# Attention on one core: the last-but-one head's normalisation is split over two engines, and the last full pair is stored in one piece

## The chip, the cores and the metric

The kernel runs on one core of a Trainium2 chip. The metric is the device time of one execution in microseconds (us), lower is better. The engines of a core that matter here are TensorE (PE, matrix products into PSUM), VectorE (DVE), ScalarE (ACT, here the exponentials), GpSimd (POOL, casts) and SyncE (SP), from whose queue most transfers are issued. ScalarE has such a queue too (ACTq). Each engine works through its own instructions in order and waits on semaphores for the others.

## The reference

Plain softmax attention, 8 batches of 8 heads, 512 queries and 512 keys of 64 numbers each, in float32:

```python
scale = 1.0 / np.sqrt(q.shape[-1])
scores = np.einsum('bhqd,bhkd->bhqk', q, k) * scale
scores = scores - scores.max(axis=-1, keepdims=True)
attn = np.exp(scores)
attn = attn / attn.sum(axis=-1, keepdims=True)
return np.einsum('bhqk,bhkd->bhqd', attn, v)
```

The output is 8 x 8 x 512 x 64 float32, 128 KB a head.

## The kernel before

**Tiling.** The 64 heads are handled as 32 pairs g = 0 to 31 of two heads h = 0, 1. For each pair q, k and v are loaded by one transfer of 256 KB each, cast to fp16 by GpSimd, and q and k are transposed by TensorE. The scores are made transposed, keys on the partitions, in blocks of 128 keys x 512 queries; two blocks go through one exponential on ScalarE (line 579). For 16 of the 128 groups VectorE works out the exponential instead (lines 596 to 640).

**Units.** The product with v (`values`, line 680) is made in units of 128 queries: four units a head, each 128 x 65 in PSUM, where the 65th column is the sum of the exponentials, since v has a column of ones. Units are counted from 4 in the order in which the heads are multiplied. Seven units share one PSUM tile, `os[u // 7]`, which fills one bank; I call it bank 0, 1, ... 36 by that number, although two places in PSUM take turns. When a bank is complete, `reciprocal` (line 645) takes 1 / sum for its units, and `normalise` (line 650) multiplies all its units by these in one VectorE instruction into `ring`, an SBUF buffer of 112 units. `store` (line 658) sends a head of four units from the ring to memory, as soon as it is whole. The pairs in `Plan.PAIRED` go out in one 256 KB transfer when their second head is there; the others as two of 128 KB.

**The end.** The order of the heads is such that pair 30 has units 244 to 251 and the first head of pair 31 has units 252 to 255; these four are alone in bank 36 and so are a normalisation of their own. The last head, (31, 1), does not use these banks: `last_values` (line 696) makes its four units in a tile of the scores' pool, `o_last`, and `finish` (line 705) takes their reciprocals (line 709), multiplies them into `obl` (line 710) and stores that from SP's queue (line 716). `store` sends the last two heads before it, (30, 1) and (31, 0), from ScalarE's queue (`left < 2`), all others from SP's.

**What sets the order.** `Plan` simulates the engines with costs given by hand and writes a list of steps (scores, values, rec, mul, store, finish and others), sorted by time; the kernel emits its instructions in the order of this list. The layer under it adds the semaphore waits between engines, from what each instruction reads and writes. `Plan.PAIRED` is read only by `store`, not by the planner, so that the list of steps is the same before and after the change.

Of the kernel before, what the change touches and what calls it, by code (L numbers as in the profile page):

```python
# [14 lines left out]
AluOp = mybir.AluOpType  # L15


class Plan:
# [25 lines left out]
    SCALE_PORT, PRODUCT_PORT, GAP, REACH = 271, 537, 20, 5  # L44
    FIRST_LAND, LOAD, STORE, LATENCY, ISSUE = 5200, 740, 370, 2300, 470
    QUEUED, URGENT = 3500, 16
    PAIRED = (3, 13)
    RAW, QK16, NV, NU = 7, 5, 12, 112
    PAIR, DUEK, DUEV, DUEL, PRE = 3300, 2800, 4000, 7000, 0

# [357 lines left out]
def kernel(  # L408
# [7 lines left out]
    nc = tc.nc  # L416
    B, H, S, D = q.shape
    P = 128
    NI = S // P
    assert NI == 4 and D == 64 and S == 512  # L420
    scale = float(D) ** -0.5
    NP = (B * H) // 2
    ppb = H // 2
    LAST = NP - 1
# [25 lines left out]
    NU = Plan.NU  # L450
    ring = cpool.tile([P, NU, D], FP32, name="ring")
# [9 lines left out]
    os, rcs = {}, {}  # L461
# [3 lines left out]
    last = {}  # L465

    def source(src, g):
        b, h = g // ppb, 2 * (g % ppb)
        return src[b, h : h + 2].rearrange("h (p i) d -> p h i d", i=NI)
# [12 lines left out]
    def load(g, names):  # L482
        if g >= NP:
            return
        for name in names:
            src = {"q": q, "k": k, "v": v}[name]
            t = load_tile(g, name)
            nc.sync.dma_start(out=t[:, :, :, :], in_=source(src, g))
# [24 lines left out]
    def dve(ins):  # L513
        latest[:] = [ins] + latest[: Plan.REACH]
        return ins
# [23 lines left out]
    def copy(g, n=0):  # L539
        if g == 1:  # L540
            dve(
                nc.vector.tensor_copy(
                    out=tqk[g][:, n], in_=tps[g][:, n].rearrange("p i c -> p (i c)")
                )
            )
            return
        dve(
            nc.vector.tensor_copy(  # L548
                out=tqk[g][:, :, :], in_=tps.pop(g).rearrange("p n i c -> p n (i c)")
            )  # L550
        )
# [90 lines left out]
    def reciprocal(u, n):  # L642
        rcs[u] = opool.tile([P, 7, 1], FP32, tag="rc", name=f"rc_{u}")
        o, x = os[u // 7], u % 7
        dve(nc.vector.reciprocal(out=rcs[u][:, 0:n], in_=o[:, x : x + n, D : D + 1]))  # L645

    def normalise(u, n):
        o, x = os[u // 7], u % 7
        dve(
            nc.vector.tensor_tensor(  # L650
                out=ring[:, u % NU : u % NU + n, :],
                in0=o[:, x : x + n, 0:D],
                in1=rcs.pop(u)[:, 0:n].broadcast_to([P, n, D]),
                op=AluOp.mult,
            )
        )

    def store():

        g, h, u0 = heads.pop(0)  # L660
        left = 2 * NP - 1 - (u0 + NI - Plan.FIRST_UNIT) // NI
        queue = nc.scalar if left < 2 else nc.sync
        u = u0 % NU
        if g in Plan.PAIRED and h == 0:
            return
        if g in Plan.PAIRED:
            both = ring[:, u - NI : u + NI, :].rearrange("p (h i) d -> p h i d", h=2)
            queue.dma_start(out=source(out, g), in_=both)
        else:
            queue.dma_start(out=source(out, g)[:, h], in_=ring[:, u : u + NI, :])  # L670
# [34 lines left out]
    def finish():  # L705
        o = last["o"]
        ob = opool.tile([P, NI, D], FP32, tag="obl", name="obl", bufs=1)
        rc = opool.tile([P, 7, 1], FP32, tag="rc", name="rc_last")
        nc.vector.reciprocal(out=rc[:, 0:NI], in_=o[:, :, D : D + 1])
        nc.vector.tensor_tensor(  # L710
            out=ob[:, :, :],
            in0=o[:, :, 0:D],
            in1=rc[:, 0:NI].broadcast_to([P, NI, D]),
            op=AluOp.mult,
        )
        nc.sync.dma_start(out=source(out, LAST)[:, 1], in_=ob[:, :, :])

    def first_loads():
        tk = load_tile(0, "k")
        tq = load_tile(0, "q")  # L720
        for h in range(2):
            nc.scalar.dma_start(out=tk[:, h], in_=source(k, 0)[:, h])
            nc.sync.dma_start(out=tq[:, h], in_=source(q, 0)[:, h])
# [95 lines left out]
    with tc.manual_schedule():  # L819
        plan = Plan(groups, NP, 3)  # L820
        steps = plan.run()
        first_loads()
        for g, name in plan.first_loads:
            load(g, name)
        make_identity(nc, ident)
        for n in range(NV):
            nc.vector.memset(vps[n][:, :, :, D : D + 1], 1.0)
        first_pair()
        do = {
            "transposes": transposes,  # L830
            "scores": scores,
            "values": values,
            "load": load,
            "store": store,
            "cast": cast_behind,
            "raise": raise_,
            "copy": lambda g, b: copy(g),
            "pass": pass_,
            "last": last_values,
            "finish": finish,  # L840
            "rec": lambda u, n, b: reciprocal(u, n),
            "mul": lambda u, n, b: normalise(u, n),
        }
        for what, *args in steps:
            do[what](*args)


# [28 lines left out]
```

## Time and profile before

| what | us |
|---|---|
| median of 3 runs (114.2 to 114.3) | 114.28 |
| the profiled execution | 114.39 |
| its span, first to last instruction | 112.5 |
| TensorE busy | 104.1 |
| ScalarE busy | 105.6 |
| VectorE busy | 101.2 |
| GpSimd busy | 65.2 |

The span is what the trace shows; the profiled execution is 1.9 us longer than it. Times in the rows of the trace are microseconds from the start of the span: a row of the timeline has the start, the length, the engine, the line, the operation, and what it writes and reads, with a count of instructions that were merged. A length after several merged instructions runs from the first one's start to the last one's end. A row of grouped instructions (with a vertical bar) gives the group's busy time and the mean length of one in ns, then the idle time ahead of them. The engines' names with q (ACTq, SPq) are the transfers issued there: the length is that of issuing, not of the transfer. Rows of transfers end with the size and the median us from issue to landing. A row of windows has the stretch, its length, the busy time of PE, PEld (weight loads), DVE, ACT and POOL with the count of instructions, TensorE's granted clock, the share of time in which the 16 DMA engines were busy, and GB/s.

### The profile page before, as it was taken

What the parts mean: (1) busy time and instruction counts of PE and PEld (TensorE: products, weight loads), DVE (VectorE), ACT (ScalarE), POOL (GpSimd) and SP (SyncE); (2) the same over time, 40 slices, a digit from 0 to 9 for tenths busy, and PEclk for the clock granted to TensorE, in tenths of its full rate; (3) what the DMA queues carried; (4) which work ended last, traced back from release to release, by engine and by line L of the source; (5) the groups of instructions that cost most, each with busy time, mean ns of one, the idle gap of its engine ahead of it and who ended that gap; (6) DMA issues with size and microseconds to landing.
All of it is one profiled execution on the core that took longest, in us unless ns stands there. A gap on an engine that the chain in (4) does not pass through costs nothing.

```text
span 112.5 us, 4339 instructions
## 1 busy us (share of the span) xinstructions
PE 104.1 (93%) x1687; PEld 69.4 (62%) x1687; DVE 101.2 (90%) x226; ACT 105.6 (94%) x118; POOL 65.2 (58%) x127
## 2 busy tenths in 40 slices
PE   7988889899999998999999999999999999999970
PEld 2554546576775565657677557678567765776560
DVE  1547999999989999999999999999999999999760
ACT  4689999999999999999999999999999999999960
POOL 2165798265478866686847888755868796000000
PEclk9999999999999999999999999999999999999999
DMA  3999999999999999999999999999999886848435
GB/s 99 301 304 359 349 349 345 351 340 346 348 342 335 313 326 355 349 353 365 324 359 348 319 300 328 340 339 312 337 338 283 277 267 207 269 145 273 154 100 182
DMA packets 35349, 33.84 MB, mean 301 GB/s; under 512 B 2560, under 2 KB 35328, under 8 KB 35328
## 3 DMA queue, kind: packets, MB, share of 16 engines
q1 hardware_dynamic: 34752, 33.04, 91.4%
q10 hardware_dynamic: 576, 0.52, 1.4%
q8 instruction: 13, 0.21, 0.9%
q14 instruction: 8, 0.07, 0.2%
HBM read 25.17 MB, written 8.39 MB: 298 GB/s over the span
## 4 chain that ended last, share of the span: by engine, by line
DVE 45%; PE 42%; ACT 7%; issue 2%; DMA 1%
PE o L680 18%; PE st L575 14%; DVE pd L599 10%; DVE tqk L548 8%; DVE ring L650 8%; ACT pt L579 7%; PE tp L535 6%; DVE m L633 4%; DVE pd L639 3%; PE st_0a L727 3%; DVE pe L625 3%; DVE m L616 2%; DVE m L635 2%; DVE rc L645 2%; DMA out_dram<-ring 1%
## 5 line engine op out<-in xcount | busy, mean ns | idle before, releaser
L579 ACT ACTIVATE pt<-st 128x1024 f16<-128x1024 f32 (+1 forms) x110 | 100.3, 1111 | 0.0
L680 PE MATMUL o<-vp,pt 128*128 128x65 f16 x880 | 46.3, 194 | 0.1
L680 PEld LDWEIGHTS <-pt 128*128 128x128 f16 x880 | 38.9, 98 | 12.2 <-issue 10.6
L575 PE MATMUL st<-tqk 64*128 64x512 f16 (+1 forms) x250 | 42.4, 381 | 2.9 <-ACT pt L579 1.7
L504 POOL CAST qkp<-k 128x512 f16<-128x512 f32 x31 | 21.7, 701 | 12.1 <-DMA k<-in_k_dram 5.2
L494 POOL CAST vp<-v 128x512 f16<-128x512 f32 x32 | 21.9, 700 | 7.9 <-DVE rc L645 2.9
L504 POOL CAST qkp<-q 128x512 f16<-128x512 f32 x30 | 21.4, 712 | 6.6 <-DVE rc L645 3.1
L650 DVE TENSOR_TENSOR ring<-o,rc 128x448 f32<-128x448 f32 (+2 forms) x37 | 22.3, 606 | 0.6
L680 PE MATMUL o<-vp,pe 128*128 128x65 f16 x128 | 22.1, 195 | 0.0
L680 PE MATMUL o<-vp,pd 128*128 128x65 f16 x128 | 21.9, 193 | 0.0
L548 DVE COPY tqk<-tp 128x1024 f16<-128x1024 f16 x30 | 20.3, 677 | 0.2 <-PE tp L535 0.2
L535 PE MATMUL tp<-ident,qkp 128*128 128x128 f16 x248 | 19.5, 219 | 0.9 <-DVE ring L650 0.7
L599 DVE TENSOR_SCALAR pd<-st 128x1024 uint16<-128x1024 f32 x16 | 19.5, 1217 | 0.7 <-PE st L575 0.7
L575 PEld LDWEIGHTS <-tqk 64*128 64x128 f16 x250 | 11.8, 93 | 12.3 <-issue 4.8
L535 PEld LDWEIGHTS <-qkp 128*128 128x128 f16 x248 | 14.3, 97 | 7.3 <-issue 4.1
L680 PEld LDWEIGHTS <-pe 128*128 128x128 f16 x128 | 12.5, 97 | 3.8 <-issue 2.9
L680 PEld LDWEIGHTS <-pd 128*128 128x128 f16 x128 | 12.6, 98 | 0.0
L639 DVE TENSOR_TENSOR pd<-pd,m 128x1024 f16<-128x1024 f16 x16 | 10.9, 682 | 0.0
L633 DVE TENSOR_TENSOR m<-m 128x1024 f16<-128x1024 f16 x16 | 10.9, 681 | 0.0
L645 DVE RECIPROCAL rc<-o 128x7 f32<-128x7 f32 (+2 forms) x37 | 7.2, 196 | 1.9 <-PE o L680 1.9
L625 DVE TENSOR_SCALAR pe<-pd 128x1024 uint16<-128x1024 uint16 x16 | 6.8, 422 | 0.0
L616 DVE TENSOR_SCALAR m<-pd 128x1024 uint16<-128x1024 uint16 x16 | 6.6, 412 | 0.0
(50 smaller groups left out, 34.5 us busy)
## 6 DMA issues: line engine op xcount, KB each, us to landing
v<-in_v_dram SPq DMA_DIRECT2D x32, 256.0 KB, 5.7
k<-in_k_dram SPq DMA_DIRECT2D x31, 256.0 KB, 5.8
q<-in_q_dram SPq DMA_DIRECT2D x31, 256.0 KB, 5.8
out_dram<-ring SPq DMA_DIRECT2D x57, 128.0 KB, 3.4
out_dram<-ring SPq DMA_DIRECT2D x2, 256.0 KB, 3.5
k<-in_k_dram ACTq DMA_DIRECT2D x2, 128.0 KB, 2.9
q<-in_q_dram SPq DMA_DIRECT2D x2, 128.0 KB, 2.7
out_dram<-ring ACTq DMA_DIRECT2D x2, 128.0 KB, 2.0
```

The costliest lines, as they stand in the source:

```text
L494: return nc.gpsimd.tensor_copy(out=vps[g % NV][:, :, :, 0:D], in_=raw[g]["v"][:, :, :, :])
L504: return nc.gpsimd.tensor_copy(out=dst, in_=src[:, :, :, :])
L535: reads[g] = nc.tensor.transpose(tps[g][:, n, i, :], qkp[g][:, n, i, :], ident)
L548: nc.vector.tensor_copy(out=tqk[g][:, :, :], in_=tps.pop(g).rearrange("p n i c -> p n (i c)"))
L575: nc.tensor.matmul(st[:, x, cols], kc, qc[:, cols], start=True, stop=True)
L579: nc.scalar.activation(out=pt[:, :, cols], in_=st[:, :, cols], func=EXP, scale=scale, bias=SHIFT)
L599: nc.vector.tensor_scalar(out=r["pd"][:, :, :], in0=r["st"][:, :, :], scalar1=BITS, scalar2=BIAS, op0=AluOp.mult, op1=AluOp.add,)
L625: ins = nc.vector.tensor_scalar(out=r["pe"][:, :, :], in0=u[:, :, :], scalar1=0x7C00, scalar2=None, op0=AluOp.bitwise_and,)
L633: ins = nc.vector.tensor_tensor(out=m16, in0=m16, in1=m16, op=AluOp.mult)
L639: ins = nc.vector.tensor_tensor(out=u16, in0=u16, in1=m16, op=AluOp.mult)
L650: nc.vector.tensor_tensor(out=ring[:, u % NU : u % NU + n, :], in0=o[:, x : x + n, 0:D], in1=rcs.pop(u)[:, 0:n].broadcast_to([P, n, D]), o ...
L680: nc.tensor.matmul(os[u // 7][:, u % 7, :], part[:, y * P : (y + 1) * P], vps[g % NV][:, h, c, :], start=(n == 0), stop=(n == len(parts) - 1),
```

## The change

In `normalise` the last bank's four units, 252 to 255, are no longer one instruction. ScalarE multiplies the first two, each by its own reciprocal, one instruction each. VectorE multiplies the third at once. The fourth is kept back and emitted in `finish`, between the last head's reciprocal and its multiply. Pair 30 takes the place of pair 13 in `PAIRED`: it goes out in one transfer of 256 KB, from SP's queue, since `left < 1` leaves only head (31, 0) on ScalarE's; pair 13 goes out in two transfers. The store of the last head is emitted behind all steps of the list instead of in `finish`. Lines of the changed file: 665 the ScalarE multiplies, 650 the single VectorE multiplies, 670 the multiply of a whole bank, 688 and 690 the stores, 729 and 732 `finish`, 868 the last store.

```diff
-    PAIRED = (3, 13)
+    PAIRED = (3, 30)
...
+    def one_unit(u, i):
+        def do_it():
+            dve(
+                nc.vector.tensor_tensor(
+                    out=ring[:, (u + i) % NU, :],
+                    in0=os[u // 7][:, u % 7 + i, 0:D],
+                    in1=rcs[u][:, i, :].broadcast_to([P, D]),
+                    op=AluOp.mult,
+                )
+            )
+
+        return do_it
+
     def normalise(u, n):
         o, x = os[u // 7], u % 7
+        if u + n == Plan.FIRST_UNIT + 8 * NP - NI:
+
+            for i in range(n // 2):
+                nc.scalar.mul(ring[:, (u + i) % NU, :], o[:, x + i, 0:D], rcs[u][:, i, :])
+            last["units"] = [one_unit(u, i) for i in range(n // 2, n)]
+            last["units"].pop(0)()
+            return
...
-        queue = nc.scalar if left < 2 else nc.sync
+        queue = nc.scalar if left < 1 else nc.sync
...
         nc.vector.reciprocal(out=rc[:, 0:NI], in_=o[:, :, D : D + 1])
+        for unit in last["units"]:
+            unit()
         nc.vector.tensor_tensor(
             out=ob[:, :, :],
             in0=o[:, :, 0:D],
             in1=rc[:, 0:NI].broadcast_to([P, NI, D]),
             op=AluOp.mult,
         )
-        nc.sync.dma_start(out=source(out, LAST)[:, 1], in_=ob[:, :, :])
+        last["ob"] = ob
...
         for what, *args in steps:
             do[what](*args)
+        nc.sync.dma_start(out=source(out, LAST)[:, 1], in_=last["ob"][:, :, :])
```

## The prediction

> **What bounds the kernel now.** I read the core's clock first, then the page's totals, then the timeline of each engine from 105 us on, because the change lies almost wholly behind the last exponentials.
>
> ```profile
> core 0: 112.5 us, clock 1.000
> PE 104.1 (93%) x1687; PEld 69.4 (62%) x1687; DVE 101.2 (90%) x226; ACT 105.6 (94%) x118; POOL 65.2 (58%) x127
> 106.18 0.20 DVE L645 RECIPROCAL rc<-o 128x7 f32<-128x7 f32 x1 [0.59 <-PE o L680]
> 107.94 0.20 DVE L645 RECIPROCAL rc<-o 128x7 f32<-128x7 f32 x1 [0.89 <-PE o L680]
> 108.18 0.62 DVE L650 TENSOR_TENSOR ring<-o,rc 128x448 f32<-128x448 f32 x1
> 108.72 0.17 DVE L645 RECIPROCAL rc<-o 128x4 f32<-128x4 f32 x1
> 108.92 0.42 DVE L650 TENSOR_TENSOR ring<-o,rc 128x256 f32<-128x256 f32 x1
> 109.27 0.17 DVE L709 RECIPROCAL rc_last<-o_last 128x4 f32<-128x4 f32 x1
> 109.47 0.42 DVE L710 TENSOR_TENSOR obl<-o_last,rc_last 128x256 f32<-128x256 f32 x1
> 106.51 2.11 ACT L579 ACTIVATE pt<-st 128x1024 f16<-128x1024 f32 x3
> 108.83 0.90 ACTq L670 DMA_DIRECT2D out_dram<-ring  x2
> 107.07 2.09 SPq L670 DMA_DIRECT2D out_dram<-ring  x3
> 109.92 0.33 SPq L716 DMA_DIRECT2D out_dram<-obl  x1
> 108.25 0.73 PE L696 MATMUL o_last<-vp,pt 128*128 128x65 f16 x16
> ```
>
> For 105 us TensorE, ScalarE and VectorE are all above 90% busy and the change adds nothing there but one DMA. The end is a chain on VectorE. ScalarE's last exponential ends at 106.51 + 2.11 = 108.62; TensorE's last product for the last head ends at 108.25 + 0.73 = 108.98. From 107.94 VectorE does six instructions without a hole: reciprocal and multiply of bank 35 (units 245 to 251), reciprocal and multiply of bank 36 (units 252 to 255, the last-but-one head), reciprocal and multiply of the last head. The last-head reciprocal starts at 109.27, 0.08 before the multiply ahead of it ends (108.92 + 0.42 = 109.34), and 0.29 after its own input was done. So it stands in VectorE's queue, not behind TensorE. The last multiply ends at 109.89, its store is issued at 109.92.
>
> ```profile
> 107.07 1.66 DMA out_dram<-ring
> 108.73 0.17 DVE rc L645
> ```
>
> These two rows of the chain of waits put the bank-36 reciprocal down to a store. I do not follow them: it starts 0.08 before the multiply ahead of it ends, as the last-head one does, so it stood in the same queue.
>
> ```profile
> out_dram<-ring SPq DMA_DIRECT2D x3, 128.0 KB, 2.0
> out_dram<-ring ACTq DMA_DIRECT2D x2, 128.0 KB, 2.0
> out_dram<-obl SPq DMA_DIRECT2D x1, 128.0 KB, 1.8
> 109.00:110.00 1.00, 0.00 (x0) 0.00 (x0) 0.86 (x3) 0.00 (x0) 0.00 (x0) 1.00 0.49 165
> 110.00:111.00 1.00, 0.00 (x0) 0.00 (x0) 0.00 (x0) 0.00 (x0) 0.00 (x0) 1.00 1.04 340
> 111.00:112.50 1.50, 0.00 (x0) 0.00 (x0) 0.00 (x0) 0.00 (x0) 0.00 (x0) 0.99 0.15 50
> ```
>
> The last store lands 1.8 after its issue, at 111.7, and 0.8 of barrier follows. In the windows (last two numbers: DMA share, GB/s) the transfers are full from 110 to 111 and nearly empty after: the last store runs close behind the ones before it, but is not far from free.
>
> The profiled execution took 114.39 us, 1.9 more than its span; the median of the three runs, 114.28, is 0.1 below it. I work out a shift of the span and add it to the median.
>
> **The change, part by part.**
>
> *Two units on ScalarE, one on VectorE, then the last head.* The 0.42 multiply of bank 36 goes. ScalarE gets two multiplies of 64 elements, reading bank 36 of PSUM and its reciprocals; VectorE gets one of 64 ahead of the last-head reciprocal, and one between that and the last multiply. The point on which all turns is a wait. In the changed program as built, the first single multiply on VectorE waits for ScalarE's counter at the value that the second of the two ScalarE multiplies sets; the first of the two sets nothing. So ScalarE's pair and VectorE's unit do not run side by side but one after the other, and the last-head reciprocal, in the same queue behind the waiting unit, is late with it, and so are the second unit, the last multiply and its store.
>
> [...]
>
> The price needs ScalarE and VectorE instructions of a size that the trace before lacks, so I go by its nearest rows:
>
> ```profile
> 4.02 0.41 ACT L745 CAST q<-q 128x256 f16<-128x256 f32 x1 [0.32 <-DMA q<-in_q_dram]
> 4.33 0.40 ACT L746 CAST k<-k 128x256 f16<-128x256 f32 x1
> 5.16 0.60 ACT L777 ACTIVATE pt<-st_0a 128x512 f16<-128x512 f32 x1 [0.43 <-PE st_0a L770]
> 5.66 0.59 ACT L777 ACTIVATE pt<-st_0b 128x512 f16<-128x512 f32 x1
> 107.41 1.21 ACT L579 ACTIVATE pt<-st 128x512 f16<-128x512 f32 x2
> L579 ACT ACTIVATE pt<-st 128x512 f16<-128x512 f32 x2 | 1.2, 726 | 0.0
> L579 ACT ACTIVATE pt<-st 128x1024 f16<-128x1024 f32 x108 | 99.3, 1118 | 0.0
> L743 ACT ACT_TABLE_LOAD x1 | 1.3, 1283 | 1.7 <-PEq L860 1.7
> L650 DVE TENSOR_TENSOR ring<-o,rc 128x448 f32<-128x448 f32 x35 | 21.6, 618 | 0.5
> L650 DVE TENSOR_TENSOR ring<-o,rc 128x256 f32<-128x256 f32 x1 | 0.4, 424 | 0.0
> L650 DVE TENSOR_TENSOR ring<-o,rc 128x192 f32<-128x192 f32 x1 | 0.4, 351 | 0.0
> ```
>
> VectorE: 448, 256 and 192 elements cost 618, 424 and 351 ns, about 1.03 ns an element; 64 elements come to 0.22 us. ScalarE: 512 elements take 0.60 and start 0.50 apart (5.16, 5.66), 256 take 0.40 and start 0.31 apart (4.02, 4.33). In line with these, 64 elements take 0.25 and start 0.17 apart: 0.42 for the pair. Lower end: the two late exponentials start 1.21 - 0.73 = 0.48 apart, and from 512 to 1024 elements one grows by 392 ns, 0.77 an element, so 64 would start 0.14 apart and the pair could be done in 0.14 + 0.22, say 0.33. Upper end: no overlap and the 0.40 of the cast each, 0.80. All these rows take their scale as a constant, where the multiply reads one per partition, so I take 0.46, a little above the nearest pair.
>
> [...]
>
> Now the sum. The bank-36 reciprocal ends at 108.72 + 0.17 = 108.89 as before. ScalarE has been free since 108.62 and starts 0.05 later, 108.94 (hand-overs in the first rows: multiply end 108.80 to ScalarE's DMA issue 108.83; multiply end 109.89 to SP's issue 109.92). The pair ends at 109.40. VectorE's unit starts at 109.44. Its end, 109.66, less the 0.08 by which VectorE instructions without a wait overlap, puts the last-head reciprocal at 109.58 (before: 109.27). It ends at 109.75; the second unit starts at 109.67 and ends at 109.89; the last multiply needs the reciprocal (109.75 + 0.03) and the queue (109.89 - 0.08) and starts at 109.81, where it was 109.47. **Shift: +0.34 us.** With the pair at 0.33 or 0.80 it is +0.21 or +0.68.
>
> Had the wait not been there, VectorE's first unit would start at 108.92, the reciprocal at 109.06 (its input is done at 108.98), the last multiply at 109.29: -0.18.
>
> *The stores at the end.* Before, (30,0) left on SP and (30,1) on ScalarE's queue, both when bank 35 was done (108.80), and (31,0) on ScalarE's queue behind. Now pair 30 is one 256 KB store on SP, issued at 108.83, and only (31,0) is left on ScalarE. It waits for VectorE's second unit, 109.89, is issued at 109.92 and lands 2.0 later, 111.9. The last store is issued at 109.81 + 0.42 + 0.03 = 110.26 and lands 1.8 later, 112.06: still last. The pair store lands by 111.2, if it takes 0.4 longer than the 2.0 of a single one; I cost it at nothing, covered by 0.8. That the last store is now emitted behind all steps costs nothing either: SP's queue holds only the pair store ahead of it, issued a microsecond before. Whether the last store lands in 1.8 is open: the one before it is now 0.34 ahead instead of half a microsecond, but pair 30 has drained by then. I take no change, with 0.1 either way.
>
> *Pair 13 leaves in two stores.* One more issue on SP at about 87 us:
>
> ```profile
> 87.04 0.41 SPq L668 DMA_DIRECT2D out_dram<-ring  x1
> 87.55 0.45 SPq L488 DMA_DIRECT2D v<-in_v_dram  x1
> ...
> L494 POOL CAST vp<-v x32: 607/626/1017, 9.0 to 93.8; 128x512 f16<-128x512 f32 x32
> ```
>
> Behind it in SP's queue stands the last load, v of pair 30, about 0.4 later than at 87.55. Its cast, among the last of those up to 93.8, has until the first unit of pair 30, the last unit of bank 34, whose reciprocal waits for TensorE at 106.18. Over 10 us of cover; cost nothing, and +0.4 if the cover were gone.
>
> **The rivals.** (About 0.2%, 0.23 us, is what a measurement of this kernel can tell from no change: 114.05 to 114.51 is the same.)
>
> 1. *The wait costs nothing.* ScalarE's pair would have to be done when VectorE comes to its unit, by 108.9; then the chain is 0.18 shorter: 114.10, and 114.0 if the last store also finds the transfers free. Against it: the pair cannot start before 108.89, where the reciprocals end. Only a ScalarE pair of less than about 0.12 (0.34 less of it than taken) breaks even, and the shortest pair I could draw from the rows is 0.33.
> 2. *A short pair.* At 0.33 the shift is 0.21: 114.49, told by the measurement from nothing at best barely. For it: the lower line above. Against: the scale that is read.
> 3. *The store of (31,0) becomes the late one.* It and the last store, 0.34 apart, carry 128 KB each; at the 340 GB/s of the windows that is 0.39 a store, so the second may wait 0.05 to 0.1 on the first: 114.72. For it: ScalarE's stores took 2.0, the last one 1.8.
> 4. *A table load before the first multiply*, 1283 ns as in the row: 115.9. Against: the program as built has one load, at the start.
> 5. *The stores of pair 13 delay something*: up to 114.7. Against: the cover above.
>
> **How the numbers follow.** Forecast, the serial chain: 0.66, 114.62, its own range 114.50 to 114.80. Rival 1: 0.06 (most of it faster, the rest the same); rival 2: 0.15; rival 3: 0.09; rivals 4 and 5: 0.02 each. Slower: 0.66 + 0.09 + 0.04 = 0.79; same: 0.15 and the rest of rival 1, 0.17; faster: 0.04. The range runs from 114.40 (the short pair with the last store 0.1 quicker) to 114.95 (the upper pair, 0.68); outside it are rival 1, rival 4 and the tails.
>
> **What would show it.** In the changed kernel's timeline: two ScalarE instructions of 128x64 from about 108.94, end near 109.40; VectorE's first 128x64 multiply starting only behind them, with idle time put down to ScalarE before it, where VectorE had none; the last-head reciprocal near 109.58 and the last multiply near 109.81; the last store issued near 110.26, landing after 1.8. If VectorE's first single multiply starts near 108.92, the forecast is wrong at its root. If the order holds and the time is off, it is the pair's length or the landing of the last store. Any difference before 105 us would speak for rival 5.

## The result and the profile after

| | before | after |
|---|---|---|
| median, us (22 runs each) | 114.29 | 114.71 |
| lowest to highest, us | 113.68 to 115.43 | 114.07 to 115.70 |
| ratio, 95% interval | | 1.0042, 1.0023 to 1.0062 |
| the profiled execution, us | 114.39 | 115.06 |
| its span, us | 112.5 | 113.2 |

The change costs 0.48 us by the ratio (0.26 to 0.71 by its interval). The forecast was 114.62, slower. Medians and ratios here and below leave out the executions that ran slow, two of `e5_vector_alone` (116.41 and 132.25, at a lower clock) and three of the kernel before.

The two profiled executions differ by 0.66 in span, more than the change can be charged with. The exponentials of the execution after are 0.24 later than before by 26 us and 0.26 at the last; nothing of the change has happened by 26 us, and in the executions of the other kernels this offset lies anywhere from -0.27 to +0.65 by then. So the tail is read from a mark that both kernels reach in the same way: the start of the reciprocal of bank 36, called R below (108.72 before, 108.98 after). R stands at the same distance behind the start of the last exponential, to within 0.01, in all executions profiled here but two; those two are of one kernel (`e7_early_store`, run again as `e11_early_again`), whose edit puts it 0.065 later. Where an experiment takes two reciprocals for bank 36, R is the start of the first.

First the cores view and the page's totals of the kernel after, then its timeline of VectorE, ScalarE and SyncE.

```profile
core 0: 113.2 us, clock 0.999
PE 103.4 (91%) x1687; PEld 68.5 (61%) x1687; DVE 101.1 (89%) x227; ACT 106.2 (94%) x120; POOL 65.5 (58%) x127
108.44 0.62 DVE L670 TENSOR_TENSOR ring<-o,rc 128x448 f32<-128x448 f32 x1
108.98 0.17 DVE L645 RECIPROCAL rc<-o 128x4 f32<-128x4 f32 x1
109.74 0.23 DVE L650 TENSOR_TENSOR ring<-o,rc 128x64 f32<-128x64 f32 x1 [0.59 <-ACT ring L665]
109.88 0.17 DVE L729 RECIPROCAL rc_last<-o_last 128x4 f32<-128x4 f32 x1
109.97 0.19 DVE L650 TENSOR_TENSOR ring<-o,rc 128x64 f32<-128x64 f32 x1
110.08 0.42 DVE L732 TENSOR_TENSOR obl<-o_last,rc_last 128x256 f32<-128x256 f32 x1
106.77 2.12 ACT L579 ACTIVATE pt<-st 128x1024 f16<-128x1024 f32 x3
109.19 0.52 ACT L665 ACTIVATE ring<-o,rc 128x64 f32<-128x64 f32 x2 [0.29 <-DVE rc L645]
110.24 0.34 ACTq L690 DMA_DIRECT2D out_dram<-ring  x1
109.09 0.38 SPq L688 DMA_DIRECT2D out_dram<-ring  x1
110.54 0.33 SPq L868 DMA_DIRECT2D out_dram<-obl  x1
```

The row to look at is the third of VectorE: 0.59 of idle time, ended by ScalarE. VectorE's reciprocal ends at 109.15, ScalarE's two multiplies run from 109.19 to 109.71 beside an idle VectorE, and only then the single multiply starts, at 109.74. The last head's reciprocal, in the same queue, is late with it (0.90 behind R; before 0.55), then the last multiply (1.11 behind R; before 0.75), then its store. The chain of waits now begins inside this stretch:

```profile
109.71 0.02 issue
109.74 0.23 DVE ring L650
109.96 0.09 DVE rc_last L729
110.05 0.11 DVE ring L650
110.16 0.35 DVE obl L732
```

All it has is VectorE and 0.02 of issue ahead of it; the chain stops at 109.71, the end of ScalarE's second multiply.

The last three transfers of the kernel after (operation, count, size, us from issue to landing), and then by windows of half a microsecond, the last two numbers being the DMA engines' busy share and GB/s:

```profile
out_dram<-ring SPq DMA_DIRECT2D x1, 256.0 KB, 2.1
out_dram<-ring ACTq DMA_DIRECT2D x1, 128.0 KB, 1.7
out_dram<-obl SPq DMA_DIRECT2D x1, 128.0 KB, 1.8
110.25:110.75 0.50, 0.00 (x0) 0.00 (x0) 0.26 (x1) 0.00 (x0) 0.00 (x0) 1.00 1.01 342
110.75:111.25 0.50, 0.00 (x0) 0.00 (x0) 0.00 (x0) 0.00 (x0) 0.00 (x0) 1.00 0.33 109
111.25:111.75 0.50, 0.00 (x0) 0.00 (x0) 0.00 (x0) 0.00 (x0) 0.00 (x0) 1.00 1.01 344
111.75:112.25 0.50, 0.00 (x0) 0.00 (x0) 0.00 (x0) 0.00 (x0) 0.00 (x0) 1.00 0.28 92
```

Windows of the kernel before:

```profile
109.50:110.00 0.50, 0.00 (x0) 0.00 (x0) 0.40 (x1) 0.00 (x0) 0.00 (x0) 1.00 0.65 219
110.00:110.50 0.50, 0.00 (x0) 0.00 (x0) 0.00 (x0) 0.00 (x0) 0.00 (x0) 1.00 1.03 336
110.50:111.00 0.50, 0.00 (x0) 0.00 (x0) 0.00 (x0) 0.00 (x0) 0.00 (x0) 1.00 1.05 344
111.00:111.50 0.50, 0.00 (x0) 0.00 (x0) 0.00 (x0) 0.00 (x0) 0.00 (x0) 1.00 0.45 150
```

Before, the transfers run without a hole from 110.00 until the last one is through. After, there is a hole at 110.75 to 111.25: pair 30 has gone and head (31, 0) is not there yet. Both readings come back below, with the experiments' numbers in one table (us behind R, one profiled execution each; a kernel's last landing is that of the transfer that ends last):

| kernel | last multiply starts | its store issued | last landing | end of span |
|---|---|---|---|---|
| before | 0.75 | 1.21 | 2.97 | 3.81 |
| after | 1.11 | 1.56 | 3.37 | 4.21 |
| `e1_stores_only` | 0.75 | 1.20 | 3.02 | 3.85 |
| `e2_split_only` | 1.11 | 1.56 | 3.37 | 4.21 |
| `e3_other_bank` | 0.61 | 1.06 | 3.02 | 3.86 |
| `e4_pair_twice` | 1.52 | 1.97 | 3.78 | 4.62 |
| `e5_vector_alone` | 0.75 | 1.20 | 3.01 | 3.84 |
| `e6_unit_behind` | 0.51 | 0.97 | 3.07 | 3.91 |
| `e7_early_store` | 0.61 | 1.66 | 3.61 | 4.45 |
| `e8_both_pairs` | 1.11 | 1.56 | 3.37 | 4.26 |
| `e9_late_load` | 0.76 | 1.21 | 3.07 | 3.91 |
| `e10_bank_only` | 0.61 | 1.06 | 2.96 | 3.80 |
| `e11_early_again` | 0.61 | 1.06 | 2.94 | 3.78 |

Total times scatter by almost 2 us from run to run, so that the ratios below resolve some 0.3 to 0.5 us. The distances from R resolve more, but not all alike. The start of the last multiply repeats within 0.005 in kernels that have the same code up to there, and the reading of the wait rests on it. The landings and the end do not repeat as well: the end of `e9_late_load` is programmed as before, and still comes 0.10 later (3.91 against 3.81); `e8_both_pairs` ends 0.05 behind the changed kernel with the same landing. So differences of less than 0.1 in the last two columns are not taken for an effect.

### The profile page after: what moved, and what is told of

Same layout as the page of the kernel before. It is cut to its first block, busy times and chain, and to the rows that moved or that the text cites. A ratio compares the mean times of both kernels' runs of the same rounds, so it can differ in the third digit from the quotient of the medians.

```text
span 113.2 us, 4342 instructions
## 1 busy us (share of the span) xinstructions
PE 103.4 (91%) x1687; PEld 68.5 (61%) x1687; DVE 101.1 (89%) x227; ACT 106.2 (94%) x120; POOL 65.5 (58%) x127
## 5 line engine op out<-in xcount | busy, mean ns | idle before, releaser
L670 DVE TENSOR_TENSOR ring<-o,rc 128x448 f32<-128x448 f32 (+1 forms) x36 | 21.9, 611 | 0.5
```

Source lines behind the costliest of these rows:

```text
L670: nc.vector.tensor_tensor(out=ring[:, u % NU : u % NU + n, :], in0=o[:, x : x + n, 0:D], in1=rcs.pop(u)[:, 0:n].broadcast_to([P, n, D]), o ...
```

## The experiments

The theory on trial is the forecast's: VectorE's unit waits for ScalarE's second multiply, and everything behind it in VectorE's queue is late by that wait. That it waits since all four units lie in one PSUM bank is a guess, which `e3_other_bank` tries. The rivals are that the new stores do it, or that pair 13's two stores delay something 25 us earlier. Diffs are against the changed kernel, or against the one that the sentence names.

**The two halves of the change, each alone.**

`e1_stores_only` has the new stores and the old normalisation:

```diff
     def normalise(u, n):
         o, x = os[u // 7], u % 7
-        if u + n == Plan.FIRST_UNIT + 8 * NP - NI:
-            ...
-            return
...
-        for unit in last["units"]:
-            unit()
```

> The stores as changed (pair 30 in one, pair 13 in two, last store emitted last), bank 36 multiplied by VectorE in one instruction as before. Measured in the tail: from the last exponential's end to the span's end it was 3.90 before and 4.30 in the changed kernel; from the bank-36 reciprocal's start to the last multiply's start 0.75 and 1.10. Theory W (VectorE waits for ScalarE's pair): 0.75 and a tail of 3.85 to 3.95, time within 0.2% of before. Rival S (the stores cost it): tail 4.2 to 4.3, time 0.3 to 0.4% above before. Rival M (many small instructions cost it, with or without a wait): as theory W here.

`e2_split_only` has the new normalisation and the old stores:

```diff
-    PAIRED = (3, 30)
+    PAIRED = (3, 13)
...
-        queue = nc.scalar if left < 1 else nc.sync
+        queue = nc.scalar if left < 2 else nc.sync
```

> The normalisation split as changed, the stores of pairs 13 and 30 as before, so that (30, 1) leaves from ScalarE's queue behind the two multiplies. Theory W: 1.10 from the bank-36 reciprocal to the last multiply, tail 4.25 to 4.40 (the store of (30, 1) is issued 0.6 later than before and may delay the last by up to 0.1), time 0.3 to 0.45% above before. Rival S: tail 3.9, time as before. Rival M: as theory W here.

Measured: the stores alone 114.52 against 114.28, ratio 1.0024 (0.9989 to 1.0059), the end 0.04 further behind R, which is within the scatter. The split alone 114.70 against 114.28, ratio 1.0039 (1.0011 to 1.0068), the end 0.40 further behind R, which is all of what the whole change has (4.21 in both). So the split is the cause, and the stores add nothing to it that these executions show.

**The wait taken away.** `e3_other_bank` gives units 252 and 253 a PSUM tile of their own, from the scores' pool, so that ScalarE and VectorE read different banks. The reciprocal of bank 36 becomes two of two units each.

```diff
+    FAR = Plan.FIRST_UNIT + 8 * NP - 2 * NI
...
+        if u == FAR:
+            dve(nc.vector.reciprocal(out=rcs[u][:, 0:2], in_=last["far"][:, 0:2, D : D + 1]))
+            dve(nc.vector.reciprocal(out=rcs[u][:, 2:n], in_=o[:, x + 2 : x + n, D : D + 1]))
+            return
...
-                nc.scalar.mul(ring[:, (u + i) % NU, :], o[:, x + i, 0:D], rcs[u][:, i, :])
+                nc.scalar.mul(ring[:, (u + i) % NU, :], last["far"][:, i, 0:D], rcs[u][:, i, :])
...
+        dst = os[u // 7][:, u % 7, :]
+        if u == FAR:
+            last["far"] = ps_st.tile([P, 2, S], FP32, tag="st", name="o_far")[
+                :, 0, 0 : 2 * (D + 1)
+            ].rearrange("p (x d) -> p x d", x=2)
+        if FAR <= u < FAR + 2:
+            dst = last["far"][:, u - FAR, :]
...
-                os[u // 7][:, u % 7, :],
+                dst,
```

> As changed, but units 252 and 253, ScalarE's, are made in a PSUM bank of their own (a free tile of the scores), so that VectorE's single multiply has no wait for ScalarE; one more small reciprocal. Theory W: the first single multiply starts 0.30 after the first of the two reciprocals' start, without idle time put down to ScalarE; the last multiply 0.64 after it instead of 1.10; tail 3.80, 0.5 below the changed kernel and 0.1 below before; time 0 to 0.2% below before. Rival M: the last multiply stays 0.9 to 1.1 behind, tail 4.1 to 4.3. Rival S: tail 4.2 to 4.3.

VectorE and ScalarE in the timeline of `e3_other_bank`:

```profile
108.48 0.16 DVE L648 RECIPROCAL rc<-o_far 128x2 f32<-128x2 f32 x1
108.56 0.15 DVE L649 RECIPROCAL rc<-o 128x2 f32<-128x2 f32 x1
108.75 0.22 DVE L656 TENSOR_TENSOR ring<-o,rc 128x64 f32<-128x64 f32 x1
109.09 0.42 DVE L745 TENSOR_TENSOR obl<-o_last,rc_last 128x256 f32<-128x256 f32 x1
108.68 0.52 ACT L671 ACTIVATE ring<-o_far,rc 128x64 f32<-128x64 f32 x2 [0.28 <-DVE rc L648]
```

With two banks, VectorE's unit starts at 108.75 without an idle stretch, while ScalarE's pair runs until 109.20. The last multiply starts 0.61 behind R, 0.50 sooner than in the changed kernel and 0.15 sooner than before. So the wait comes from the units of both engines sharing bank 36. (That bank is one tile, `os[36]`, and the pair's new place is another, so this run does not tell whether the layer that adds the waits goes by the bank or by the tile.) But the end did not follow: the last store was issued 0.15 sooner than before and landed no sooner (3.02 against 2.97), and the time was 114.31 against 114.28 (ratio 1.0009, 0.9979 to 1.0039). What the chain won, the transfers took; `e10_bank_only` below tests this.

**The wait made longer.** `e4_pair_twice` does ScalarE's pair twice:

```diff
-            for i in range(n // 2):
+            for i in 2 * list(range(n // 2)):
```

> As changed, but ScalarE makes its two multiplies twice over, the second pair on top of the first: the wait is doubled, VectorE's work is the same. Theory W: VectorE's first single multiply 0.5 to 0.55 later than in the changed kernel, the last multiply 1.60 to 1.65 behind the bank-36 reciprocal instead of 1.10, tail 4.8 to 4.85, time about 0.9% above before. Rivals M and S: as the changed kernel, 1.10 and 4.30.

ScalarE and VectorE in the timeline of `e4_pair_twice`:

```profile
109.60 0.93 ACT L665 ACTIVATE ring<-o,rc 128x64 f32<-128x64 f32 x4 [0.30 <-DVE rc L645]
110.56 0.22 DVE L650 TENSOR_TENSOR ring<-o,rc 128x64 f32<-128x64 f32 x1 [1.00 <-ACT ring L665]
```

Four multiplies take 0.93, two take 0.52, and VectorE's wait grows by the same 0.41 (0.59 to 1.00), the end of the span by 0.41 (4.21 to 4.62); 115.38 against 114.32, ratio 1.0072 (1.0031 to 1.0112). The second pair adds 0.41 and not another 0.52, as 0.5 to 0.55 had been expected, since multiplies in a row overlap: they take 0.31 to 0.32 each and start 0.20 to 0.21 apart. What ScalarE's work grew by, the end grew by.

**The pair on VectorE.** `e5_vector_alone` keeps the pieces and the stores, but lets VectorE multiply units 252 and 253 in one instruction:

```diff
-            for i in range(n // 2):
-                nc.scalar.mul(ring[:, (u + i) % NU, :], o[:, x + i, 0:D], rcs[u][:, i, :])
+            dve(
+                nc.vector.tensor_tensor(
+                    out=ring[:, u % NU : u % NU + 2, :],
+                    in0=o[:, x : x + 2, 0:D],
+                    in1=rcs[u][:, 0:2].broadcast_to([P, 2, D]),
+                    op=AluOp.mult,
+                )
+            )
```

> As changed, but ScalarE's two units are multiplied by VectorE in one instruction of 128 elements ahead of its single unit: as many small instructions in VectorE's queue as changed and one more, no wait. Theory W: the last multiply 0.70 to 0.75 behind the bank-36 reciprocal, tail 3.85 to 3.95, time within 0.2% of before. Rival M: 0.9 or more, tail 4.1 or more. Rival S: tail 4.2 to 4.3.

The last multiply starts 0.75 behind R as in the kernel before, and the end stands where the stores alone put it (3.84; `e1_stores_only` 3.85). Cutting the multiply into three costs nothing; only the second engine does. Time: 114.41 against 114.32, ratio 1.0012 (0.9972 to 1.0052).

**The last head first.** `e6_unit_behind` gives ScalarE three units and moves VectorE's single unit behind the last head's multiply, so that nothing of the last head waits for ScalarE:

```diff
-            for i in range(n // 2):
+            for i in range(n - 1):
...
-            last["units"] = [one_unit(u, i) for i in range(n // 2, n)]
-            last["units"].pop(0)()
+            last["units"] = [one_unit(u, i) for i in range(n - 1, n)]
...
-        for unit in last["units"]:
-            unit()
         nc.vector.tensor_tensor(
...
         last["ob"] = ob
+        for unit in last["units"]:
+            unit()
```

> Three units on ScalarE, the fourth on VectorE behind the last multiply, so that nothing ahead of the last multiply waits for ScalarE. Theory W: the last multiply 0.50 to 0.55 after the bank-36 reciprocal (bound by TensorE's last product), the last head's store issued 0.2 to 0.25 earlier than before in the tail; the store of (31, 0) becomes the last to land, tail 3.8 to 3.9; time 0 to 0.1% below before. Rival M: the last multiply 0.75 or more behind. Rival S: tail 4.2 or more whatever the multiply does.

The last head's store is issued 0.24 sooner than before and lands 0.27 sooner (2.70), but now (31, 0) is last and lands at 3.07: 114.56 against 114.28, ratio 1.0024 (0.9990 to 1.0057). With nothing of the last head behind ScalarE, the last of the four heads lands at about 3.0 behind R, whichever it is.

**What holds the end once the wait is gone.** `e10_bank_only` is `e3_other_bank` with the stores of the kernel before:

```diff
-    PAIRED = (3, 30)
+    PAIRED = (3, 13)
...
-        queue = nc.scalar if left < 1 else nc.sync
+        queue = nc.scalar if left < 2 else nc.sync
```

> The changed kernel with units 252 and 253 in a bank of their own, so that no unit waits for ScalarE, and with the stores as before (pair 13 in one, pair 30 in two). If VectorE's chain were the bound of the end: last store issued 0.15 earlier than before (1.06 us behind the start of bank 36's reciprocal) and landing 0.15 earlier, some 2.82 behind it, total about 114.13. If the transfers of the last four heads, back to back, hold the end: landing at 2.97 to 3.02 as in the kernel before, total the same within 0.05.

The windows of `e10_bank_only`, read as above, and its last transfer:

```profile
110.50:111.00 0.50, 0.00 (x0) 0.00 (x0) 0.00 (x0) 0.00 (x0) 0.00 (x0) 1.00 1.04 344
111.00:111.50 0.50, 0.00 (x0) 0.00 (x0) 0.00 (x0) 0.00 (x0) 0.00 (x0) 1.00 1.02 338
111.50:112.00 0.50, 0.00 (x0) 0.00 (x0) 0.00 (x0) 0.00 (x0) 0.00 (x0) 1.00 0.72 236
out_dram<-obl SPq DMA_DIRECT2D x1, 128.0 KB, 1.9
```

The transfers are full from 110.50 until the last is through, with no hole, and the last store takes 1.90 from issue to landing where it took 1.76 before. Issued 0.15 sooner, it landed 0.01 sooner; 114.43 against 114.48, ratio 1.0002 (0.9968 to 1.0036). The landings of (30, 1), (31, 0) and the last head stand at 2.23, 2.59 and 2.96 behind R, in the kernel before at 2.23, 2.61 and 2.97: 0.36 to 0.37 apart, a little less than the 0.39 that 128 KB take at the 340 GB/s of the windows. Its tail is as short as that of the kernel before, and so is its time.

The other direction shows in `e9_late_load` (described under pair 13), whose end is programmed as in the kernel before. Two of SyncE's issues in its timeline, the second of them the store of (30, 0), and two of its windows:

```profile
107.47 1.43 SPq L670 DMA_DIRECT2D out_dram<-ring  x1
108.99 0.38 SPq L670 DMA_DIRECT2D out_dram<-ring  x1
109.50:110.00 0.50, 0.00 (x0) 0.00 (x0) 0.41 (x1) 0.00 (x0) 0.00 (x0) 1.00 1.04 346
111.00:111.50 0.50, 0.00 (x0) 0.00 (x0) 0.00 (x0) 0.00 (x0) 0.00 (x0) 1.00 0.71 236
```

In the kernel before, the first of these issues took 0.79 and its store landed 0.96 behind R. Here it took 1.43 and the store landed only at 1.66, and the store of (30, 0) was issued 0.15 later. So the transfers had one store more to move ahead of the last ones: they were full from 109.50 on, where the kernel before had a share of 0.65 there, and had more left at the end (0.71 against 0.45). The last multiply stood where it did before (0.76 and 0.75 behind R), but the last three stores landed at 2.35, 2.73 and 3.07, each 0.10 to 0.12 later, and the end came 0.10 later. So here the transfers moved the end with VectorE's chain unchanged.

**The train of transfers started sooner.** `e7_early_store` is `e3_other_bank` with pair 13 in one store again and pair 30 in two, both from SyncE, and with bank 35 multiplied in two pieces, so that head (30, 0) can leave after the first:

```diff
-    PAIRED = (3, 30)
+    PAIRED = (3, 13)
...
+        cut = 3 if u + n == FAR else n
+        for a, b in ((0, cut), (cut, n)):
+            ...
```

> ScalarE's units in a bank of their own, as in the run of that name, and bank 35 multiplied in two instructions (units 245 to 247, then 248 to 251), so that the store of (30, 0) can leave about 0.27 earlier; pair 30 in two stores from SP's queue, pair 13 in one as before. Theory T (with the wait gone the transfers of the last four heads hold the end): the transfers start 0.25 earlier against the bank-36 reciprocal, the last store lands 1.70 to 1.80 after its issue instead of 1.96, span end 3.60 to 3.70 after the start of the bank-36 reciprocal (before 3.81, the other-bank run 3.86), of which 0.07 is given back, since two instructions for bank 35 put that reciprocal 0.07 later; time 0 to 0.2% below before. If the end is not held by the transfers: 1.96 again, 3.85.

It missed: the end stood at 4.45. SyncE's issues and the last multiply in the timeline of `e7_early_store` (the first row is the first of the four issues that the second row sums up):

```profile
107.03 1.82 SPq L701 DMA_DIRECT2D out_dram<-ring  x1
107.03 3.27 SPq L701 DMA_DIRECT2D out_dram<-ring  x4
110.39 0.41 SPq L886 DMA_DIRECT2D out_dram<-obl  x1
109.34 0.42 DVE L750 TENSOR_TENSOR obl<-o_last,rc_last 128x256 f32<-128x256 f32 x1
```

The last multiply ended at 109.76, but one issue of SyncE had taken 1.82 from 107.03, and the stores behind it followed one after the other until 110.30; the last one was issued at 110.39. The same kernel ran again as `e11_early_again`:

> The kernel of e7_early_store again. If SyncE's backlog at the end was an accident of that execution: its queue is caught up by about 104 us, the last store is issued at once behind its multiply (1.05 us behind the start of bank 36's reciprocal) and lands 2.9 to 3.0 behind it; span end 3.75 to 3.85. If it belongs to the kernel: the last store is issued at about 1.66 again, span end near 4.45.

```profile
107.23 1.42 SPq L701 DMA_DIRECT2D out_dram<-ring  x2
108.75 0.98 SPq L701 DMA_DIRECT2D out_dram<-ring  x2
110.00 0.33 SPq L886 DMA_DIRECT2D out_dram<-obl  x1
```

Here the same four issues were through at 109.73, and the last store went out 0.03 behind its multiply; the end came at 3.78 (one run, 114.49; the runs before beside it 114.48). That is the end expected without the backlog, but not the 3.60 to 3.70 of theory T: R is 0.065 later in this kernel, so against the exponentials nothing was won. The first store of the train, (30, 0), landed 0.32 sooner than before (1.71 against 2.03), but (30, 1), now behind it in SyncE's queue, was issued only at 0.41 and landed at 2.21 (before 2.23); from there on the landings are those of before. That a train started sooner as a whole would end sooner is therefore not shown. The backlog itself did not come again, but this kernel is open to it: over 12 runs `e7_early_store` took 114.65 against 114.29, ratio 1.0023 (0.9999 to 1.0046). How often it happens is not known.

**Pair 13.** In `e1_stores_only` and `e5_vector_alone`, where pair 13 leaves in two stores, the exponentials came later by 0.22 and 0.11 from 102 us on, which spoke for the rival of the forecast. Two runs test it. `e8_both_pairs` joins pair 13 again in the changed kernel:

```diff
-    PAIRED = (3, 30)
+    PAIRED = (3, 13, 30)
```

> The changed kernel with pair 13 in one store again (pairs 3, 13 and 30 in one). Theory W: the tail as changed, 1.10 from the bank-36 reciprocal to the last multiply, end 4.2 after that reciprocal. Theory P (pair 13 in two stores makes the last v load late, its cast falls beside a VectorE pass and stretches it): here the last load issues no later than before against the exponentials (87.2 to 87.6 on the time scale of before), its cast does not wait for the transfer, no jump of the exponentials' offset after 95 us; time 0.1 us below the changed kernel. Without P: the issue of that load scatters as in the runs with pair 13 in two, 86.7 to 90.1.

`e9_late_load` is the kernel before with the last load of v put behind three more stores in SyncE's queue:

```diff
+        at = steps.index(("load", 30, "v"))
+        late = steps.pop(at)
+        behind = [n for n, x in enumerate(steps) if x[0] == "store" and n >= at][2]
+        steps.insert(behind + 1, late)
```

> The kernel before with one edit: the last load, v of pair 30, stands three stores later in SP's queue, so that it is issued about 1.3 to 2.5 later; its values are needed only at 104.9. Theory P: its cast waits for the transfer, falls beside the VectorE pass at 94.88 (0.42 there), which takes 0.53 to 0.65 instead; all exponentials from 102 us on are 0.1 to 0.25 later against the earlier ones; time 0.1 to 0.2% above before. Without P: no jump, time as before.

`e8_both_pairs` took 114.98 against 114.29, ratio 1.0057 (1.0029 to 1.0084), with the last multiply at 1.11 as in the changed kernel: nothing is won by joining pair 13, and its last load was issued at 89.4 on the scale of before, no sooner than where pair 13 leaves in two. In `e9_late_load` the load was issued 3.45 later, and no exponential was late; 114.41 against 114.29, ratio 1.0020 (0.9989 to 1.0052). What made the two steps shows in the timeline around 94 us, ahead of the exponentials that moved: the last cast of v on GpSimd against a pass of VectorE over 16-bit data (line 635). `e1_stores_only`:

```profile
94.34 0.62 POOL L494 CAST vp<-v 128x512 f16<-128x512 f32 x1 [1.02 <-DMA v<-in_v_dram]
94.59 0.64 DVE L635 TENSOR_SCALAR m<-m 128x1024 f16<-128x1024 f16 x1
```

`e9_late_load`:

```profile
94.89 0.42 DVE L635 TENSOR_SCALAR m<-m 128x1024 f16<-128x1024 f16 x1
94.96 0.82 POOL L494 CAST vp<-v 128x512 f16<-128x512 f32 x1 [1.34 <-DMA v<-in_v_dram]
```

In these rows the one that starts second takes longer. In `e1_stores_only` the cast begins ahead of the pass, the pass takes 0.64 instead of 0.42 (0.53 in `e5_vector_alone`) and VectorE loses 0.22 (0.11), which the exponentials then show; in `e9_late_load` the pass begins first, the cast takes 0.82 instead of 0.62 and nobody waits for it. In `e7_early_store` the cast begins only 0.14 ahead of the end of the pass, and takes its 0.62. In the changed kernel's own execution the pass took 0.42. Put on the scale of the kernel before, the load of v is issued between 87.4 and 89.7 in the six executions that have pair 13 in one store and the load in its old place, and between 86.7 and 90.1 in the six that have it in two. So the rival is not borne out as a cause of the result; whether two stores make the collision somewhat more frequent, these runs can't say.

## Why the prediction was right, and where it was not

- **The wait.** Right at its root: VectorE's first single multiply began 0.03 behind the end of ScalarE's second, with 0.59 idle ahead of it, and with another bank (`e3_other_bank`) the wait was gone. Why the layer puts two engines' reads of one bank in order, no run here shows.
- **ScalarE's pair.** Forecast 0.46, measured 0.52 (0.31 each, starts 0.21 apart), within the range of 0.33 to 0.80. Mis-sized by 0.06: from casts of 256 elements I had taken a 64-element instruction for 0.25. The 0.04 put on top of the nearest pair (0.42) for a scale read per partition was an estimate, and no run here measures that part by itself.
- **The hand-overs.** Forecast 0.05 and 0.04, in the rows 0.04 and 0.03. VectorE's units took 0.23 and 0.19 (forecast 0.22 each). Together this gave back most of the pair's excess: the last multiply came 0.35 later (1.106 - 0.754), forecast 0.34. The mechanism was right; that its terms cancel to 0.01 is luck.
- **The last store's landing.** "No change, with 0.1 either way": it went from 1.76 to 1.82 behind the issue, 0.05, within that margin. What rival 3 describes does run: (31, 0) finds the transfers free and lands 1.74 behind its issue; the last store is issued 0.30 behind it and lands 0.37 behind it, 1.81 to 1.82 behind its own issue in four executions (after, `e2_split_only`, `e4_pair_twice`, `e8_both_pairs`). But the last store of the kernel before was not free either: 1.76 in its own execution, 1.86 in `e9_late_load`. So the store does wait on the one ahead, as rival 3 says, and whether the change added to that is not shown.
- **The sum.** 0.35 + 0.05 = 0.40 in the tail, where `e2_split_only` has it too; against the tail of `e9_late_load` it would be 0.30. The runs say 0.48, 0.26 to 0.71, which holds both. Whether the rest is more than scatter is not to be told at this interval.
- **Rival 1, "-0.18 without the wait", 114.10.** The chain on VectorE would have won 0.15 (`e3_other_bank`, `e10_bank_only`), near the 0.18; the time would have won nothing. What fails in it is what it draws from the reading "the last store runs close behind the ones before it, but is not far from free". At its own time of issue the store was nearly free, 1.76 against 1.74, but it also landed 0.36 behind (31, 0), the distance at which stores land here that follow one another without a hole. VectorE's chain and the transfers ended together in the kernel before, so the later chain cost its full price and a sooner one gained nothing.
- **The pair store "costed at nothing".** Right in this kernel: its landing, 2.26 behind R, is 1.11 ahead of the last, and `e2_split_only` without it ends at the same 4.21. But the cover is the hole that the wait makes. Without the wait (`e1_stores_only`, `e3_other_bank`) the last stores follow it without a hole, and it lands 0.05 to 0.06 later there than (30, 1) did from a queue of its own (before, `e10_bank_only`); the end is later by as much, which is less than the scatter.
- **Pair 13, "over 10 us of cover".** Wrong in its working: values are indeed not wanted before 104.9 us, but a late cast that ran into VectorE's pass cost 0.22 in `e1_stores_only` and 0.11 in `e5_vector_alone`. It did not happen in the changed kernel's profile, so it has no share in the reading above.
- **What would show it.** "Any difference before 105 us would speak for rival 5" was too wide: there was a difference of 0.24 already by 26 us. It should have said a step in the offset behind 87 us.

## What to carry to other kernels

In this kernel, work given to a second engine ran beside the first only when the two read different PSUM banks, each a tile of its own (0.59 of idle time on VectorE with one bank, none with two in `e3_other_bank`): look first at where the operands lie, and price work that waits like this as one chain, with a hand-over at each end (0.04 and 0.03 here). At the end of a kernel, compare the landings of the last transfers with the time one of them takes: if they follow one another without a hole, as here at 0.35 to 0.38 us for 128 KB, a shorter chain of compute alone gains nothing (in `e10_bank_only` the last store was issued 0.15 sooner and landed 0.01 sooner). And where total times scatter by more than the effect, measure distances from a mark in the trace that both kernels reach alike, and take from two executions of like code how well such a distance repeats.

## What was not expected of the hardware

- The last three stores land 0.35 to 0.38 apart in seven executions (before, `e1_stores_only`, `e3_other_bank`, `e5_vector_alone`, `e9_late_load`, `e10_bank_only`, `e11_early_again`), whatever the distance of their issues (0.30 to 0.55 between the last two). The store of (31, 0), where it finds the transfers free, lands 1.74 to 1.75 behind its issue (after, `e2_split_only`, `e4_pair_twice`, `e8_both_pairs`).
- Where GpSimd's cast and VectorE's 16-bit pass overlap, the second can take longer: the pass 0.64 and 0.53 instead of 0.42 (`e1_stores_only`, `e5_vector_alone`), the cast 0.82 in `e9_late_load` and 1.01 in the kernels before and after instead of 0.62. The pass, when second, ended 0.28 behind the cast's end in both executions that show it; the cast, when second, ended 0.47 to 0.48 behind the pass's end in the eleven others, in two behind line 635 and in nine behind line 633.
- Most issues of a store take SyncE 0.33 to 0.45, but of the 60 or so of an execution five to ten take 0.6 to 2.0. One of them stands near 107 us in all thirteen executions: 0.79 in the kernel before, 0.87 after, 1.43 in `e9_late_load`, 1.82 in `e7_early_store` and 1.04 in the same kernel's other execution. What makes them long was not followed up; it goes with 0.10 at the end of `e9_late_load` and 0.67 at that of `e7_early_store` (4.45 against 3.78).
